# A two-round mixer trunk on one core: the second round's first head as two Strassen quads in turn, and a later gate for the last convolution group

## The chip, the cores and the metric

The kernel runs on one core of a Trainium2 chip. Its five engines are TensorE (PE, matmuls), VectorE (DVE), ScalarE (ACT), GpSimd (POOL) and SyncE (SP, which here issues transfers). The metric is the device time of one execution in microseconds. Before the change the median of three runs is 867.72 us.

## The reference

One layer of a hybrid trunk, all in fp32, for 2048 rows behind 16 meta tokens:

```python
hn = rms_norm(h, norm_g)
proj = hn @ w_in                                   # (rows, 1024) x (1024, 8*512)
cx, cb, cc, cg, q, k, v, rg = split(proj, 8)
conv_out = cb * causal_conv3(cc * cx) * silu(cg)   # 4 groups of 128 channels
q, k = rotary(q) * 128**-0.5, rotary(k)            # 4 heads of 128
ret = head_group_norm(retention_chunkwise(q, k, v), ret_norm_g)   # chunks of 128
mixed = concat(conv_out, ret * silu(rg))
out = rms_norm(h + mixed @ w_out, final_g)
```

## The kernel before

**Rounds and units.** The 2048 rows are worked in two rounds of 1024 (`NR`), and each round goes through eight units, four heads (0 to 3) and four convolution groups (4 to 7), in the order of `UNITS` (L37): round 0 starts with group 4, round 1 with head 0, and both end with group 7. Behind them come eight output pairs of 256 rows (`output`, L943). `rr` and `rr2` are a round's row factors of the norm; they are multiplied in behind the projection.

**Quads.** A unit projects 1024 rows on 2 x 256 columns. Each half of that, a quad, is a 2 x 2 problem of blocks with four k-tiles each. A weight tile is 128 x 512, a moving tile 128 x 512 (the rows). Each fp32 product is three fp32r matmuls, high and low parts against each other, so that a block product is 4 x 3 = 12 matmuls. `quad` (L241) does the four output blocks in seven products by Strassen's scheme in Winograd's form, 84 matmuls at L252. It needs sums of blocks on both sides, four of them for the weights (`stationary`, L147) and four for the moving side. `quad_plain` (L298) does eight products without sums, 96 matmuls at L309. Only the opening group of round 0, the first quad of round 1 (K and V of head 0) and output pair 0 are plain.

**Parts.** A weight is split by ACT (cast to `wh`, L119) and DVE (`wl`, L120) into a ring of three pairs (`RING`). The moving parts `mh{i}{kt}` and `ml{i}{kt}` (operand i, k-tile kt) have one buffer each and stay for the round. For round 1, `moving` (L182) loads 16 blocks of `x` with the gain (`ml` at L123), and `prepared` (L226) loads 16 sums (`sums_x`, made in round 0) as tiles `t`. The weights' sums of round 0 are kept in DRAM (`sums_a`) for round 1. A product's bank `pj` (four in PSUM) is copied by ACT to a `tc` (L259) or taken by DVE.

**The first head of round 1.** Its first quad is handed plain weights (`first`, L1140), `between[1]` (`rest_of_sums`, L1144) makes operands 3 and 4 of the moving side behind it, and the second quad (Q, RG) follows with operands 0 to 6. In `head` (L765), `take` (L776) puts K through `rotary` (L721, four DVE products) and V through `part` (L741: ACT splits the fp32 words into 16-bit planes, a transposing DMA `cross` turns them). Of the steps of the second quad, `split_keys` sends a half of K the same way, `join` puts a turned half of V together, `weigh` scales it, and `join_keys` makes `kd` in one of the two buffers of tag `b` (`brief`, L104). All this is ACT's.

**Group 7.** The second quad of `conv_group` (L649) gives the gate's two blocks (j = 0, 1) and the two of CB. `take` (L693) adds and scales a gate block (DVE), `gated` (L687) applies Silu (ACT) and multiplies the taps `cs[j]`, tiles named `c`, by `rr` and by the gate (two POOL products, `mul` at L663). In round 0 `store` waits in `kept` and is popped in `rest_of_sums`; in round 1 it follows at once.

**What sets the order.** No order is written by hand. The tile framework runs the program against a simulated timeline and gives each engine its instructions in the order that comes out; `tc.issue_after(ins)` holds a step behind an instruction. General tiles (`gen`, 16 buffers) carry loads, `u`, `c`, `kv`, `qg` and the rest.

The central lines of the program before, at the start of round 1:

```python
m, b = moving(load_x(r), gain_of)
first = [plain_parts(w_loads(0))]
load_tables()
prepared(m, sums_x, (1, 3))

def rest_of_sums():
    prepared(m, sums_x, (0, 2))
    with tc.issue_after(loaded[0].ins):
        kept.pop()()
```

Of the kernel before, what the change touches and what calls it, by code (L numbers as in the profile page):

```python
# [15 lines left out]
P = 128  # L16
# [4 lines left out]
NG = 4  # L21
# [57 lines left out]
def hybrid_trunk(ctx: ExitStack, tc: tile.TileContext, t, out: bass.AP, chunk_decay):  # L79
# [102 lines left out]
    def moving(load, scale=None, after={}, behind={}):  # L182
# [12 lines left out]
        return m, blocks  # L195

    def block_sums(b11, b12, b22, b21, t1, t3, f, g):
# [14 lines left out]
        sub(nc.vector, t3, b22, b11)  # L212
# [28 lines left out]
    def quad(w, m, take, steps=()):  # L241
# [42 lines left out]
        product(6, xb, False)  # L284
        take(1, 0, xb, None)

    def plain_part(n, load, slot):
# [151 lines left out]
    def row_factors(r, f):  # L439

        f.extend([row_tile("rr", r), row_tile("rr2", r), []])
        rows = load_rows(r, 0)
# [114 lines left out]
    def kept_sums(n, r):  # L557
        return sums_a[n] if r == 0 and n in KEPT else None

    mixed = [  # L560
# [88 lines left out]
    def conv_group(g, r, m, f, blocks, ahead, steps=(), last=False):  # L649
# [35 lines left out]
        gates = []  # L685

        def gated():  # L687
            j, c = gates.pop()
            nc.scalar.activation(c, c, AF.Silu)  # L689
            mul(nc.gpsimd, cs[j], cs[j], rr[j])  # L690
            mul(nc.gpsimd, cs[j], cs[j], c)

        def take(i, j, pp, c):  # L693
            if i == 0:
                add(nc.vector, c, pp, c)
# [44 lines left out]

    def part(a, to_cross=None):  # L741

        apart, across = gen("pl")[:, :HB], gen("tr")[:, :HB]
        nc.scalar.copy(out=planes(apart), in_=halves(a))
        if to_cross is None:
            cross(across, apart)
        else:
            to_cross.append((across, apart))
        return across
# [15 lines left out]
    def head(h, r, m, rot_t, f, turning, blocks, ahead, sums, first=(), between=((), idle, idle, idle)):  # L765
# [3 lines left out]

        to_cross, queried = [], []  # L770
        k, v, late = [None, None], [None, None], []
# [3 lines left out]

        def take(i, j, pp, c):  # L776
            if i == 1 and c is None:
                v[j] = part(pp, to_cross if len(first) else None)
                return
# [11 lines left out]

        if len(first) > 0:
            quad_plain(first[0], m, take)
        else:
            with tc.issue_after(spreading[0].ins) if r + h == 0 else nullcontext():
                w = stationary(blocks[0], nc.vector if r + h == 0 else nc.gpsimd, kept_sums(2 * h, r))
            quad(w, m, take, between[0] or (finish_late,))
            catch_up(0)
        between[1]()
        if to_cross:  # L800
            with tc.issue_after(loaded[0].ins):
                for pair in to_cross:
                    cross(*pair)
        q, sg = [None, None], [None, None]

        def take(i, j, pp, c):
            d = gen("qg")[:, :HB]
# [23 lines left out]

        def split_late():
            for j in late:
                v[j] = part(v[j])
            split_keys(0)

# [18 lines left out]

        quad(stationary(load_raw(w_loads(2 * h + 1, r)), keep=kept_sums(2 * h + 1, r)), m, take, (split_late, middle, late_middle))
        with tc.issue_after(copied[0].ins):
            join(1)
            weigh(1)
            join_keys(1)  # L860
        between[2]()
        with tc.issue_after(queried[0].ins):
# [80 lines left out]
    def output(pair, m, final_g):  # L943
# [111 lines left out]
    for r in range(NR):  # L1055
# [82 lines left out]
        else:  # L1138
            m, b = moving(load_x(r), gain_of)
            first = [plain_parts(w_loads(0))]  # L1140
            load_tables()
            prepared(m, sums_x, (1, 3))

            def rest_of_sums():  # L1144
                prepared(m, sums_x, (0, 2))
                with tc.issue_after(loaded[0].ins):
                    kept.pop()()

            between = (), rest_of_sums, idle, idle
            blocks = None, None  # L1150
# [5 lines left out]
        for n, unit in enumerate(units):  # L1156
# [67 lines left out]
```

## Time and profile before

| | |
|---|---|
| runs | 867.62, 867.72 and 867.89 us |
| profiled execution | 867.66 us, its span 865.9 us |
| PE | 854.1 us busy, 99% of the span, 4216 matmuls |
| DVE | 683.0 us, 79% |
| ACT | 499.0 us, 58% |
| POOL | 288.7 us, 33% |
| chain that ended last | PE 93%, DVE 3% |
| granted clock of PE | 0.998 on the mean |

Times run from the span's start. A busy PE row is a matmul's length as it is modelled, and neighbouring rows overlap; the distance between their starts is what PE spends on one. The first head of round 1 begins at about 360 us, and the output at about 710 us. "Released by" names what ended the idle time before an instruction.

### The profile page before, as it was taken

Reading aid. Unit: us, or ns where it says so; the run is one execution under the profiler, and the core shown is the slowest. Engines: PE = TensorE matmul, PEld = TensorE weight load, DVE = VectorE, ACT = ScalarE, POOL = GpSimd, SP = SyncE. Lnnn points to the kernel's source line nnn. Section 1 sums busy time; section 2 is a strip of 40 time slices with the busy share of each in tenths; the row PEclk is TensorE's granted clock in tenths of the full one; section 3 lists DMA queues with packets and bytes.
Section 4 is the critical chain, followed back from the end, with each engine's and each line's share of the span. In section 5 each row is a group of like instructions: output and inputs, shape, how many; then the busy total and the mean of one; then the engine's idle time right before and its main releaser. Section 6 shows DMA issues by size and latency. Waiting matters only on the chain.

```text
span 865.9 us, 12846 instructions
## 1 busy us (share of the span) xinstructions
PE 854.1 (99%) x4216; PEld 705.7 (82%) x4216; DVE 683.0 (79%) x1204; ACT 499.0 (58%) x901; POOL 288.7 (33%) x226
## 2 busy tenths in 40 slices
PE   8999999999999999999999999999999999999996
PEld 6778888878887778788888888888888888888885
DVE  6798989889897977979677787976655699767663
ACT  7875648474855654948374757544433565555553
POOL 0022232422255554320000002341312154777773
PEclk9999999999999999999999999999999999999999
DMA  8736357566777744966365657547344584455441
GB/s 294 252 142 159 96 145 210 149 185 193 183 233 242 243 147 158 338 197 163 81 171 178 162 194 167 186 135 256 97 122 122 205 318 146 162 181 169 146 139 68
DMA packets 141187, 154.43 MB, mean 178 GB/s; under 512 B 59904, under 2 KB 77632, under 8 KB 141120
## 3 DMA queue, kind: packets, MB, share of 16 engines
q1 hardware_dynamic: 140544, 153.21, 57.8%
q8 instruction: 33, 0.54, 0.3%
q10 hardware_dynamic: 576, 0.40, 0.1%
q14 instruction: 34, 0.28, 0.1%
HBM read 101.14 MB, written 39.85 MB: 163 GB/s over the span
## 4 chain that ended last, share of the span: by engine, by line
PE 93%; DVE 3%; issue 1%; DMA 1%; POOL 0%; ACT 0%; POOLq 0%; SPq 0%; DVEq 0%
PE pj L252 75%; PE pj L309 5%; PE pj L333 5%; PE ms L902 2%; PE ms L891 2%; PE ms L901 2%; PE ms L878 2%; PE ms L506 1%; DVE wl L120 1%; DMA ra<-in_w_in 1%; DVE ml L123 0%; DMA gain<-in_norm_g 0%; DVE qg L931 0%; DVE x L205 0%; DVE c L581 0%
## 5 line engine op out<-in xcount | busy, mean ns | idle before, releaser
L252 PE MATMUL pj<-mh,wl 128*128 128x512 f32 x1008 | 395.7, 393 | 0.5 <-DVE wl L120 0.5
L252 PE MATMUL pj<-mh,wh 128*128 128x512 f32 x1008 | 393.2, 390 | 0.0
L252 PE MATMUL pj<-ml,wh 128*128 128x512 f32 x1008 | 392.7, 390 | 0.0
L119 ACT CAST wh<-ra 128x512 fp32r<-128x512 f32 x229 | 142.3, 621 | 250.3 <-PE pj L252 210.6
L120 DVE TENSOR_TENSOR wl<-ra,wh 128x512 fp32r<-128x512 f32 x229 | 188.3, 824 | 59.4 <-ACT wh L119 58.2
L252 PEld LDWEIGHTS pj<-mh,wl 128*128 128x128 f32 x1008 | 189.3, 188 | 41.1 <-issue 1.1
L252 PEld LDWEIGHTS pj<-mh,wh 128*128 128x128 f32 x1008 | 189.3, 188 | 39.4
L252 PEld LDWEIGHTS pj<-ml,wh 128*128 128x128 f32 x1008 | 189.4, 188 | 38.1
L131 POOL TENSOR_TENSOR ra<-ra 128x512 f32<-128x512 f32 x44 | 69.0, 1567 | 78.7 <-PE ms L506 38.3
L914 POOL TENSOR_TENSOR rp<-rs,neg_half 128x4 f32<-128x4 f32 x16 | 18.8, 1173 | 151.5 <-DVE rs L128 151.4
L259 ACT COPY tc<-pj 128x512 f32<-128x512 f32 x108 | 62.6, 580 | 0.2
L128 POOL TENSOR_TENSOR sa<-ra 128x512 f32<-128x512 f32 x22 | 33.2, 1508 | 59.2 <-DMA ra<-in_w_in 38.2
L663 POOL TENSOR_TENSOR c<-c,tc 128x512 f32<-128x512 f32 x14 | 26.1, 1862 | 47.7 <-ACT tc L689 47.7
L131 POOL TENSOR_TENSOR ra<-sa,ra 128x512 f32<-128x512 f32 x22 | 31.7, 1440 | 30.5 <-DVE wl L120 20.6
L977 DVE TENSOR_TENSOR yo<-pj,yo 128x512 f32<-128x512 f32 (+1 forms) x33 | 21.9, 671 | 17.5 <-PE pj L252 8.8
L663 POOL TENSOR_TENSOR c<-c,rr 128x512 f32<-128x512 f32 x14 | 22.3, 1592 | 36.9 <-DVE c L704 25.0
L988 POOL TENSOR_TENSOR z<-yo,final_g 128x512 f32<-128x512 f32 x16 | 27.1, 1692 | 19.4 <-DVE yo L977 19.4
L128 DVE TENSOR_TENSOR tc<-pj,tc 128x512 f32<-128x512 f32 x28 | 19.2, 684 | 14.6 <-PE pj L252 14.6
L918 DVE TENSOR_SCALAR pm<-ms,mv,rp 128x128 f32<-128x128 f32 x64 | 21.8, 404 | 10.2 <-POOL rp L914 10.2
L123 DVE SCALAR_TENSOR_TENSOR ml<-x,gain,mh 128x512 fp32r<-128x512 f32 x32 | 24.7, 809 | 5.6 <-ACT mh L122 5.4
L128 POOL TENSOR_TENSOR yo<-yo,tc 128x512 f32<-128x512 f32 x18 | 26.0, 1454 | 3.4 <-ACT tc L259 3.2
L581 DVE SCALAR_TENSOR_TENSOR c<-u,conv_w,c 128x512 f32<-128x512 f32 x32 | 25.2, 830 | 2.3 <-POOL u L572 1.2
(161 smaller groups left out, 1214.0 us busy)
## 6 DMA issues: line engine op xcount, KB each, us to landing
ra<-in_w_in SPq DMA_DIRECT2D x111, 256.0 KB, 2.9
ra<-sums_a SPq DMA_DIRECT2D x52, 256.0 KB, 2.9
x<-in_xT SPq DMA_DIRECT2D x48, 256.0 KB, 5.0
sums_a<-ra SPq DMA_DIRECT2D x42, 256.0 KB, 2.1
w<-in_w_out SPq DMA_DIRECT2D x32, 256.0 KB, 5.0
ra<-mixed SPq DMA_DIRECT2D x32, 256.0 KB, 2.8
yo<-in_x SPq DMA_DIRECT2D x32, 256.0 KB, 4.4
ra<-in_x SPq DMA_DIRECT2D x16, 256.0 KB, 3.5
```

What stands on the lines that cost most here:

```text
L119: nc.scalar.copy(out=hi, in_=src)
L120: lowered[0] = eng.tensor_tensor(out=lo, in0=src, in1=hi.bitcast(F32), op=ALU.subtract)
L123: nc.vector.scalar_tensor_tensor(out=lo, in0=src, scalar=scale, in1=hi.bitcast(F32), op0=ALU.mult, op1=ALU.subtract)
L128: eng.tensor_tensor(out=out, in0=a, in1=b, op=ALU.add)
L131: eng.tensor_tensor(out=out, in0=a, in1=b, op=ALU.subtract)
L252: nc.tensor.matmul(bank, a[:, ks], b, start=first and kt == 0 and n == 0, stop=kt == KH - 1 and n == 2, skip_group_check=not first,)
L259: copied[0] = nc.scalar.copy(out=c, in_=bank)
L309: nc.tensor.matmul(banks[i], a[:, ks], b, start=half + kt + n == 0, stop=half == 1 and kt == KH - 1 and n == 2,)
L333: nc.tensor.matmul(banks[n][i], a[:, ks], b, start=half + kt + s == 0, stop=half == 1 and kt == KH - 1 and s == 2,)
L581: nc.vector.scalar_tensor_tensor(out=c, in0=u[:, tap : tap + HB], scalar=conv_w[:, g, tap : tap + 1], in1=c, op0=ALU.mult, op1=ALU.add)
L663: eng.tensor_tensor(out=out, in0=a, in1=b, op=ALU.mult)
L988: nc.gpsimd.tensor_tensor(out=ys[i][j], in0=y, in1=final_g[:, j * HB : (j + 1) * HB], op=ALU.mult)
```

## The change

**The head.** `moving` and the plain weights go at the start of round 1. `moving_in_turn` loads operands 0 and 1 of the moving side and hands back five steps that make operands 2, 3, 4, 5 and 6. The new `quads` runs both quads of head 0 product by product, K/V's and then Q/RG's, seven products each, and does a step behind each pair of products. All four banks are in use. `weights_in_turn` splits a quad's weights one by one as its products ask for them; K/V now takes its sums from `sums_a`, which Q/RG did already. Key and value splits are steps as well, and joins and weighings come behind the last product.

**Group 7.** `last` is now true in both rounds. Then the gate's addition goes to a `brief("cg")`, and nothing more is done. `gate_late` does the rest: per j a product of the gate with `rr` (DVE, L732), Silu (ACT), a product of the taps with `rr` (DVE instead of POOL, also L732), and their product (POOL). It returns `store`. Round 0's stands in the step that makes operand 6 in round 1's head (`gate_kept`), round 1's at the end of output pair 1.

```diff
+    def moving_in_turn(load, scale, sums):
...
+        blocks(0, 0)
+        blocks(1, 0)
+        steps = [
+            lambda: sums(m, 1), lambda: sums(m, 0), lambda: sums(m, 2), lambda: blocks(1, 1), lambda: sums(m, 3),
+        ]
+        return m, steps
...
+    def quads(ws, m, takes, between=()):
...
+        for i in range(7):
+            for n, take in enumerate(takes):
+                if i < 2:
+                    banks[n][i] = ps_proj()
+                bank = banks[n][1 if i in (1, 3, 5) else 0]
+                product(n, i, bank, i in (0, 1, 3))
...
+            next(between, idle)()
...
+    def weights_in_turn(n, r):
+        for load in w_loads(n, r):
+            a = raw()
+            load(a)
+            yield weight_parts(a)
...
         def take(i, j, pp, c):
             if i == 0:
+                if last:
+                    gate = brief("cg")
+                    add(nc.vector, gate, pp, c)
+                    ungated.append(gate)
+                    return
...
+        def gate_late():
+            for j, gate in enumerate(ungated):
+                mul(nc.vector, gate, gate, rr[j])
+                nc.scalar.activation(gate, gate, AF.Silu)
+                mul(nc.vector, cs[j], cs[j], rr[j])
+                mul(nc.gpsimd, cs[j], cs[j], gate)
+            return store
+
         if last:
-            kept.append(store)
+            kept.append(gate_late)
...
-        if len(first) > 0:
-            quad_plain(first[0], m, take)
...
+        if len(first) > 0:
+            steps = list(first) + [split_values, lambda: split_keys(1)]
+            steps[3] = lambda: (first[3](), split_keys(0))
+            quads([weights_in_turn(2 * h + n, r) for n in range(2)], m, (take_keys, take_queries), steps)
+            join_keys(0)
             join(1)
             weigh(1)
+            join(0)
+            weigh(0)
             join_keys(1)
+        else:
...
+        if pair == 1:
+            with tc.issue_after(last[0].ins):
+                kept.pop()()()
...
-            m, b = moving(load_x(r), gain_of)
-            first = [plain_parts(w_loads(0))]
+            m, first = moving_in_turn(load_x(r), gain_of, lambda m, n: prepared(m, sums_x, (n,)))
             load_tables()
-            prepared(m, sums_x, (1, 3))
...
+            def gate_kept(last=first[4]):
+                last()
+                with queued((loaded[0], lowered[0])):
+                    kept.pop()()()
+
+            first[4] = gate_kept
+            between = (), idle, idle, idle
...
-                blocks = conv_group(unit - NG, r, m, f, blocks, rest, FACTOR_STEPS.get(unit, ()) if r == 0 else (), r == 0 and following is None)
+                blocks = conv_group(unit - NG, r, m, f, blocks, rest, FACTOR_STEPS.get(unit, ()) if r == 0 else (), following is None)
```

**The order, first piece.** DVE late in round 1's first head, where the last moving parts and weights are made (`wl` weights, `ml30` operand 3's tile 0, `kv` and `qg` rotary products). Before:

```order
L727 TENSOR_TENSOR kv_4150<-kv_4150,rot_t_3868 128x512
L728 TENSOR_TENSOR kv_4150<-kv_4150,rot_4152 128x512
L120 TENSOR_TENSOR ml30_4163<-t_4160,mh30_4162 128x512
L120 TENSOR_TENSOR ml31_4169<-t_4166,mh31_4168 128x512
L120 TENSOR_TENSOR wl_4239<-ra_4218,wh_4238 128x512
L120 TENSOR_TENSOR ml32_4175<-t_4172,mh32_4174 128x512
L120 TENSOR_TENSOR ml33_4181<-t_4178,mh33_4180 128x512
L120 TENSOR_TENSOR ml40_4187<-t_4184,mh40_4186 128x512
```

And with the change:

```order
L814 TENSOR_TENSOR qg_4025<-qg_4025,rot_4027 128x512
L120 TENSOR_TENSOR wl_4191<-ra_4188,wh_4190 128x512
L120 TENSOR_TENSOR ml41_4105<-t_4102,mh41_4104 128x512
L120 TENSOR_TENSOR ml42_4111<-t_4108,mh42_4110 128x512
L120 TENSOR_TENSOR ml43_4117<-t_4114,mh43_4116 128x512
L123 SCALAR_TENSOR_TENSOR ml50_4163<-x_4160,gain_69,mh50_4162 128x512
L123 SCALAR_TENSOR_TENSOR ml51_4169<-x_4166,gain_69,mh51_4168 128x512
L123 SCALAR_TENSOR_TENSOR ml52_4175<-x_4172,gain_69,mh52_4174 128x512
L123 SCALAR_TENSOR_TENSOR ml53_4181<-x_4178,gain_69,mh53_4180 128x512
L120 TENSOR_TENSOR wl_4211<-ra_4208,wh_4210 128x512
```

Operands 4 and 5 now stand ahead of the weight `wl_4211`, the fifth of the Q/RG quad; before, weights and operand 3 alternated, and operand 5 had been made ahead of the head.

**The order, second piece.** DVE at the end of that head, up to the next quad's first weights (`wl_4496` before, `wl_4485` with the change; `cg` the kept gate, `c` the taps, `qg` tiles of Q and RG). Before:

```order
L128 TENSOR_TENSOR qg_4346<-pj_4254,tc_4326 128x512
L820 TENSOR_TENSOR qg_4346<-qg_4346,rr_2970 128x512
L120 TENSOR_TENSOR wl_4496<-ra_4390,wh_4495 128x512
L128 TENSOR_TENSOR qg_4361<-pj_4313,tc_4305 128x512
L120 TENSOR_TENSOR wl_4500<-ra_4392,wh_4499 128x512
L725 TENSOR_TENSOR rot_4363<-qg_4361,rot_t_3868 64x512
```

And with the change:

```order
L732 TENSOR_TENSOR cg_3790<-cg_3790,rr_360 128x512
L732 TENSOR_TENSOR c_3682<-c_3682,rr_360 128x512
L732 TENSOR_TENSOR cg_3847<-cg_3847,rr_360 128x512
L732 TENSOR_TENSOR c_3686<-c_3686,rr_360 128x512
L128 TENSOR_TENSOR qg_4306<-pj_4006,tc_4094 128x512
L120 TENSOR_TENSOR wl_4485<-ra_4379,wh_4484 128x512
L813 TENSOR_TENSOR kv_4281<-kv_4281,rot_t_3862 128x512
L891 TENSOR_TENSOR qg_4357<-pj_3935,rr_2971 128x512
L120 TENSOR_TENSOR wl_4489<-ra_4381,wh_4488 128x512
```

Four gate products at L732 now stand ahead of the last addition of Q and of the next quad's first weight.

**The order, third piece.** DVE at the turn from output pair 1 to pair 2 (`yo` a block of the output; `wl_7662` before and `wl_7653` with the change are pair 2's third weight). Before:

```order
L977 TENSOR_TENSOR yo_7454<-pj_7499,yo_7454 128x512
L1012 SCALAR_TENSOR_TENSOR yo_7452<-yo_7452,rf_7613,final_g_7198 128x512
L120 TENSOR_TENSOR wl_7662<-ra_7640,wh_7661 128x512
L128 TENSOR_TENSOR tot_7621<-so_7449 128x1
L345 TENSOR_SCALAR rs_v_7624<-tot_7621 128x1
L1012 SCALAR_TENSOR_TENSOR yo_7454<-yo_7454,rf_7623,final_g_7198 128x512
```

And with the change:

```order
L1068 TENSOR_TENSOR yo_7435<-pj_7480,yo_7435 128x512
L732 TENSOR_TENSOR cg_7011<-cg_7011,rr_2971 128x512
L732 TENSOR_TENSOR c_6933<-c_6933,rr_2971 128x512
L732 TENSOR_TENSOR cg_7068<-cg_7068,rr_2971 128x512
L732 TENSOR_TENSOR c_6937<-c_6937,rr_2971 128x512
L1106 SCALAR_TENSOR_TENSOR yo_7433<-yo_7433,rf_7604,final_g_7179 128x512
L120 TENSOR_TENSOR wl_7653<-ra_7631,wh_7652 128x512
```

The same four products of round 1's gate stand ahead of the scaling of `yo` (L1012 before, L1106 now) and of that weight.

## Rows read from the trace of the kernel before

**Rows 1.** Page, section 1: busy time and share of the span, instructions of each engine
```profile
PE 854.1 (99%) x4216; PEld 705.7 (82%) x4216; DVE 683.0 (79%) x1204; ACT 499.0 (58%) x901; POOL 288.7 (33%) x226
```

**Rows 2.** Table by stretches: PE, PEld, DVE, ACT, POOL busy us (instructions), clock, DMA share, GB/s
```profile
600.00:620.00 20.00, 20.00 (x90) 16.57 (x89) 12.65 (x18) 7.85 (x14) 4.88 (x5) 1.00 0.47 148
700.00:720.00 20.00, 20.00 (x90) 16.57 (x89) 20.00 (x25) 9.41 (x17) 10.23 (x7) 1.00 0.64 231
```

**Rows 3.** Chain of waits, 350 to 410 us: start, us, what
```profile
360.69 0.69 DVE ml L120
...
388.70 19.04 PE pj L252 x84
```

**Rows 4.** PE's timeline at the head: start, us, engine, line [idle before <-releaser]
```profile
360.02 0.39 PE L309 MATMUL pj<-mh,mh 128*128 128x512 f32 x1
361.42 0.50 PE L309 MATMUL pj<-mh,ml 128*128 128x512 f32 x1 [1.02 <-DVE ml L120]
```

**Rows 5.** DVE's timeline at the head, 353 to 376 us
```profile
353.87 0.74 DVE L123 SCALAR_TENSOR_TENSOR ml<-x,gain,mh 128x512 fp32r<-128x512 f32 x1
354.53 0.68 DVE L663 TENSOR_TENSOR tc<-tc,rr 128x512 f32<-128x512 f32 x1
355.13 0.68 DVE L120 TENSOR_TENSOR wl<-ra,wh 128x512 fp32r<-128x512 f32 x1
...
374.31 0.69 DVE L725 TENSOR_TENSOR rot<-kv,rot_t 64x512 f32<-64x512 f32 x1
...
375.72 0.75 DVE L123 SCALAR_TENSOR_TENSOR ml<-x,gain,mh 128x512 fp32r<-128x512 f32 x1
```

**Rows 6.** DVE's, POOL's timelines, 351 to 385 us; a stretch; POOL's products (min/median/max ns)
```profile
351.55 1.79 DVE L120 TENSOR_TENSOR wl<-sa,wh 128x512 fp32r<-128x512 f32 x1
...
351.05 1.74 POOL L663 TENSOR_TENSOR c<-c,rr 128x512 f32<-128x512 f32 x1 [1.64 <-DVE c L581]
...
379.81 5.16 POOL L663 TENSOR_TENSOR c<-c,tc 128x512 f32<-128x512 f32 x1 [11.02 <-ACT tc L689]
...
379.81:384.97 5.16, 5.16 (x25) 4.26 (x24) 4.01 (x7) 0.00 (x0) 5.16 (x1) 1.00 0.57 184
...
L663 POOL TENSOR_TENSOR c<-c,rr x12: 1292/1712/2346, 310.1 to 703.8; 128x512 f32<-128x512 f32 x12
L663 POOL TENSOR_TENSOR c<-c,tc x12: 1287/1296/5158, 315.7 to 713.0; 128x512 f32<-128x512 f32 x12
```

**Rows 7.** DMA issues, 372 to 412 us, then 345 to 400: KB each, us to landing
```profile
t<-sums_x SPq DMA_DIRECT2D x8, 256.0 KB, 2.8
...
t<-sums_x SPq DMA_DIRECT2D x16, 256.0 KB, 4.8
...
tr<-pl SPq DMA_TRANSPOSE x3, 3.1
```

**Rows 8.** ACT's timeline at the head's end, 397 to 404 us
```profile
397.21 0.62 ACT L119 CAST wh<-ra 128x512 fp32r<-128x512 f32 x1
397.74 0.57 ACT L259 COPY tc<-pj 128x512 f32<-128x512 f32 x1
398.21 1.35 ACT L839 COPY v<-tr 128x1024 uint16<-128x1024 uint16 x1
399.43 1.03 ACT L744 COPY pl<-kv 128x1024 uint16<-128x1024 uint16 x1
...
401.37 1.28 ACT L845 ACTIVATE v<-v,vk 128x128 f32<-128x128 f32 x4
402.55 1.34 ACT L830 COPY kd<-tr 128x1024 uint16<-128x1024 uint16 x1
```

**Rows 9.** Timelines of DVE, then PE, at the end of output pair 1
```profile
745.82 0.75 DVE L1012 SCALAR_TENSOR_TENSOR yo<-yo,rf,final_g 128x512 f32<-128x512 f32 x1 [1.09 <-POOL rf L348]
746.49 0.69 DVE L120 TENSOR_TENSOR wl<-ra,wh 128x512 fp32r<-128x512 f32 x1
...
743.41 0.39 PE L252 MATMUL pj<-mh,wl 128*128 128x512 f32 x1
```

More of the change, by code (lines that the diff above doesn't have):

```diff
@@ L195, in moving, with blocks @@
         return m, blocks
+    def moving_in_turn(load, scale, sums):
+        m = [[] for _ in range(8)]
+        def blocks(half, j):
+            for kt in range(KH):
+                k = half * KH + kt
+                parts(m, BLOCK[half][j], kt, load(k, j), scale(k) if scale else None)
+        blocks(0, 0)
[4 more added lines that the diff above has]
+        return m, steps
     def block_sums(b11, b12, b22, b21, t1, t3, f, g):
@@ L285, in quad, with product, copy @@
         take(1, 0, xb, None)
+    def quads(ws, m, takes, between=()):
+        between = iter(between)
+        banks = [[None, None] for _ in ws]
+        copies = [None for _ in ws]
+        def product(n, i, bank, first):
+            wh, wl = next(ws[n])
+            for kt in range(KH):
+                ks = slice(kt * P, (kt + 1) * P)
+                mh, ml = m[i][kt]
+                for s, (a, b) in enumerate(((wl, mh), (wh, ml), (wh, mh))):
+                    nc.tensor.matmul(
+                        bank, a[:, ks], b, start=first and kt == 0 and s == 0, stop=kt == KH - 1 and s == 2,
+                        skip_group_check=not first,
+                    )
+        def copy(bank):
+            c = sb.tile([P, HB], F32, name="tc", tag="tc", bufs=COPIES)
+            copied[0] = nc.scalar.copy(out=c, in_=bank)
+            return c
+        for i in range(7):
[4 more added lines that the diff above has]
+                product(n, i, bank, i in (0, 1, 3))
+                if i == 0:
+                    copies[n] = copy(bank)
+                elif i == 1:
+                    take(0, 0, bank, copies[n])
+                elif i == 2:
+                    copies[n] = [copy(bank)]
+                elif i == 3:
+                    copies[n].append(copy(bank))
+                elif i == 4:
+                    take(1, 1, bank, copies[n][1])
+                elif i == 5:
+                    take(0, 1, bank, copies[n][0])
+                else:
+                    take(1, 0, bank, None)
+            next(between, idle)()
     def plain_part(n, load, slot):
@@ L439, in row_factors @@
     def row_factors(r, f):
-        f.extend([row_tile("rr", r), row_tile("rr2", r), []])
+        rr2 = row_tile("rr2", r)
+        f.extend([row_tile("rr", r), rr2, []])
         rows = load_rows(r, 0)
@@ L685, in conv_group @@
         gates = []
+        ungated = []
         def gated():
+            if last:
+                return
             j, c = gates.pop()
@@ L694, in take @@
             if i == 0:
+                if last:
+                    gate = brief("cg")
+                    add(nc.vector, gate, pp, c)
+                    ungated.append(gate)
+                    return
                 add(nc.vector, c, pp, c)
@@ L739, in cross, with part @@
         )
-    def part(a, to_cross=None):
+    def part(a):
         apart, across = gen("pl")[:, :HB], gen("tr")[:, :HB]
         nc.scalar.copy(out=planes(apart), in_=halves(a))
[L745 to L748, printed above, removed]
+        cross(across, apart)
         return across
@@ L774, in head, with take_keys @@
         tables = [rot_t[:, :, j * HB : (j + 1) * HB] for j in range(2)]
-        def take(i, j, pp, c):
+        def take_keys(i, j, pp, c):
             if i == 1 and c is None:
-                v[j] = part(pp, to_cross if len(first) else None)
+                v[j] = part(pp)
                 return
@@ L790, in take, with take_queries @@
                 late.append(j)
-        if len(first) > 0:
-            quad_plain(first[0], m, take)
[L794 to L803, printed above, removed]
         q, sg = [None, None], [None, None]
-        def take(i, j, pp, c):
+        def take_queries(i, j, pp, c):
             d = gen("qg")[:, :HB]
@@ L830, in join_keys, with split_values, split_late @@
             nc.scalar.copy(out=halves(kt[j]), in_=planes(across_k[j]))
-        def split_late():
+        def split_values():
             for j in late:
                 v[j] = part(v[j])
+        def split_late():
+            split_values()
             split_keys(0)
@@ L854, in late_middle @@
             between[3]()
-        quad(stationary(load_raw(w_loads(2 * h + 1, r)), keep=kept_sums(2 * h + 1, r)), m, take, (split_late, middle, late_middle))
-        with tc.issue_after(copied[0].ins):
+        if len(first) > 0:
[3 more added lines that the diff above has]
+            join_keys(0)
             join(1)
             weigh(1)
+            join(0)
+            weigh(0)
             join_keys(1)
+        else:
+            with tc.issue_after(spreading[0].ins) if r + h == 0 else nullcontext():
+                w = stationary(blocks[0], nc.vector if r + h == 0 else nc.gpsimd, kept_sums(2 * h, r))
+            quad(w, m, take_keys, between[0] or (finish_late,))
+            catch_up(0)
+            between[1]()
+            w = stationary(load_raw(w_loads(2 * h + 1, r)), keep=kept_sums(2 * h + 1, r))
+            quad(w, m, take_queries, (split_late, middle, late_middle))
+            with tc.issue_after(copied[0].ins):
+                join(1)
+                weigh(1)
+                join_keys(1)
         between[2]()
```

7 lines of the change are left out of this document (1 added, 6 removed).

## The prediction

> **What bounds the kernel now.** I first read the page's busy shares [rows 1]: TensorE (PE) is busy for 99% of the span, VectorE (DVE) for 79%, ScalarE (ACT) for 58%, GpSimd (POOL) for 33%. A matmul's end is modelled, so I read PE by its starts. The table by stretches [rows 2] shows 90 matmuls of 512 columns in 20 us both at 600 to 620 and at 700 to 720, the second with DVE busy for all 20 us: PE keeps its pitch beside a full DVE, and a matmul taken away there is time. The granted clock is 1.00 in each stretch, the higher of the two levels (2.4 GHz), and PE does not fall idle, so the clock stays out of the sum. The pitch is in the chain of waits [rows 3]: 84 matmuls in 19.04 us, 0.2267 us each, so a product of twelve takes 2.72 us. The chain also shows the one wait of note at the change: before 361.42 it goes through DVE, not PE. PE's timeline [rows 4] has a matmul at 360.02 and the next at 361.42, released by DVE's `ml`: 1.40 less 0.23, PE lost 1.17 us. From there to 407.74 it runs through.
>
> **What goes.** (a) The first head had 96 + 84 matmuls and now has 84 + 84: 12 x 0.2267 = 2.72 us, all on the path. (b) The wait at 360.02 goes. It came because 23 matmuls of the plain quad stood ahead of the last two products of the convolution group, and their `ml` parts were late. Now those two products come first (360.02 to 365.46), and at 365.46 the head needs eight `x` parts and one weight, not sixteen and four. From 353.87 the new DVE order has eight instructions with the gain (pitch 0.66) and ten others (0.60) up to the head's first weight [rows 5]: 353.87 + 5.3 + 6.0 = 365.2, in time by 0.3. POOL's two gate products of this stretch are gone as well; the one at 351.05 held a DVE instruction back by 1.1 us, 1.79 us for a `wl` where 0.68 is usual [rows 6]. So I count all of the 1.17. The transfers (four `x` loads less, four kept sums more) cost nothing while 256 KB land in about 3 us [rows 7] and are asked for a product or more ahead. Sum of what goes: 3.9 us.
>
> **What comes, term c: weight 4 of the second quad.** The 14 products now start every 2.72 us from 365.46, K/V and Q/RG in turn, and DVE makes 13 of the 14 weights and 16 of the 28 moving parts meanwhile. Weight 3 of K/V takes the buffer of Q/RG's product 1, which ends at 365.46 + 4 x 2.72 = 376.34; with ACT's cast (0.62) and DVE's subtraction its `wl` ends at about 378.3. From there to `wl_4211` (weight 4 of Q/RG) the new order has twenty DVE instructions (the first order piece shows the last of them): fourteen at 0.60, a rotary pair of 1.41, four with the gain at 0.66 [rows 5]: 8.4 + 1.4 + 2.6 = 12.4, so 390.7. PE wants it at 365.46 + 9 x 2.72 = 389.95 and waits at least 0.8 us. Counted from the load of operand 3's first part (asked for at 375.7, behind weight 2; landed at 378.7, through ACT and DVE at 379.9; then 11.3 us on DVE) it is 1.3. I take 1.3, as the later of the two chains decides. Ends: 0.8, and 2.5 if that load takes 4.8 us, as in the crowded stretch [rows 7].
>
> **Term d: the kept gate at the end of the head.** Four products for the gate now stand on DVE ahead of the first weight of the next quad (second order piece). From the end of K/V's product 5 DVE needs 0.7 for its addition, ten instructions of 0.60 and a rotary pair: 8.1 us. PE wants that weight after three more products, 8.16 us. It is a tie, and POOL decides it, for its two gate products come in just here. A POOL product beside dense DVE work delays an instruction with two SBUF operands by up to 1.1 us [rows 6]. The first holds back the fourth gate product by 1.2; the second begins while an addition from PSUM runs and holds back the weight by 0.7: 1.9 us. Ends: 0, if POOL falls into gaps, and 2.6, the price of rival 2's first product. I take 1.9, since the order has no gap there. Behind it ACT has a key split, two weight casts, a bank copy, two joins, two weighings, a key join, a cast and a bank copy, 9.6 us [rows 8] (each 0.1 less than its row, as neighbours overlap), from 2.3 us after the head's end: 12.0 us. PE wants that bank after four products and eleven small matmuls, 12.1 us. That just holds.
>
> The Trainium skill, "SBUF — State Buffer", section "SBUF: two separate sides", says that a VectorE instruction with two SBUF inputs and a GpSimd instruction that reads SBUF exclude each other for the whole instruction, whichever starts first. The row of 1.79 us agrees. The POOL product of 5.16 us [rows 6] does not: seven DVE instructions, 4.01 us in all, ran beside it. By that rule alone term d would be 1.9 and rival 2 out; by the row rival 2 keeps a chance.
>
> **Term e: the kept gate in the output.** In round 1 the same four products go to the end of output pair 1, ahead of weight 2 of pair 2 (third order piece). Before, that `wl` ended at 747.18 [rows 9]; PE wants it at 743.41 + 2 x 2.72 = 748.85. The four, 2.4 us, fill DVE's wait of 1.09 us for `rf` and push it to 748.5: in time by 0.3. If POOL's first gate product gets in ahead of it, it is 1.1 later, and PE waits 0.8. I take 0.4, ends 0 and 0.8. The stretch that loses work, 700 to 720, gains nothing, as PE keeps its pitch there already [rows 2].
>
> **Sum:** -2.72 - 1.17 + 1.3 + 1.9 + 0.4 = -0.3 us. The profiled execution took 867.66 (span 865.9), 0.06 under the median of the runs, 867.72. So 867.4. A measurement of this kernel can tell about 0.2%, 1.7 us, from no change: this is no change.
>
> **Rivals.** 1. DVE's new work stays hidden: POOL falls where DVE waits for PE anyway, d and e are 0, and c alone stands: -3.9 + 1.3 = -2.6, 865.1 us (864.6 with c at 0.8). For it: PE does not feel a full DVE at 700 to 720 [rows 2], and a tie needs half a microsecond to vanish. Against: rows 6, and an order without gaps. It holds as long as c + d + e stay under 2.2.
>
> 2. POOL is held out instead of DVE, as in the product of 5.16 us. The key joins write the two buffers that hold the gates, so ACT's first key join waits for POOL's first product; and the stores of the gated blocks stand in SP's queue ahead of the transposed copy of the second key half. From the end of POOL's second product it is a store, three loads and that copy (3.1 us to land, rows 7; 4.8 with the issues ahead of it), then key join, weighing, cast and bank copy (3.5 us, again rows 8) until PE has its bank. So if that product ends over 3.8 us after the head does (in my count it ends before), every further microsecond is PE's. With both at 5.16 us it ends 8.7 after, PE waits 0.4 for a weight behind the first join and 4.5 for the bank, and the sum is -3.9 + 1.3 + 4.9 + 0.8 = +3.1: 870.8 us. From 7.3 us after the head's end on, the whole is slower by over 0.2%. For it: two of the 24 products of this kind from 300 us on took over 4 us; against: the medians of their two kinds are 1.71 and 1.30 [rows 6].
>
> 3. That the matmuls stay is out: PE's new order has twelve rows fewer, all at this head.
>
> **How the numbers follow.** The forecast, within 1.7 us of 867.7, gets 0.53: two firm gains against three waits, of which one is firm. Rival 1 gets 0.32, as d and e are ties and a wait can't be less than 0 but can fail to come. Rival 2 gets 0.15, milder forms with late loads included. The forecast's own range is 866.0 to 869.4. For 8 in 10 the range goes down to 864.7, nearly all of rival 1, and up to 869.3, which leaves out the far part of rival 2. So faster by over 0.2%: 0.32; within 0.2%: 0.53; slower by over 0.2%: 0.15.
>
> **What would show it.** Right: 12 matmuls fewer; no wait of PE where the head begins; one of 0.8 to 1.3 us ahead of the head's tenth product, released by `wl`; one of 1 to 2 us at the first product of the next quad, with a DVE instruction of about 1.8 us and POOL's product beside it; at most 0.8 us in output pair 2. If the head's 168 matmuls run through in 38.1 us and the next quad follows at once, rival 1 holds, and c and d fail. If a gate product on POOL takes over 4 us and PE waits for ACT's bank copy ahead of the next quad's product 4, it is rival 2. A wait for `mh` or `ml` in operands 3 or 6 of the head would say that I mis-sized the loads.

## The result and the profile after

The change makes the kernel slower: 871.49 us, median of 6 runs (869.75 to 874.14), against 867.81 before. The ratio is 1.0044, with a 95% interval from 1.0031 to 1.0057. A second batch of the same kernel gave 1.0052 (1.0035 to 1.0069). That lies outside the forecast range of 864.7 to 869.3.

The page's busy shares after the change, against [rows 1]:

```profile
PE 851.8 (98%) x4204; PEld 702.8 (81%) x4204; DVE 686.8 (79%) x1210; ACT 499.6 (58%) x901; POOL 274.8 (32%) x222
```

The twelve matmuls are gone (4216 to 4204), and with them 2.3 us of PE's busy time; but PE is busy for 98% of the span, not 99%. So the loss is waits. PE's timeline has them, as in [rows 4]: the idle time before a matmul, and what ended it.

```profile
360.32 0.50 PE L269 MATMUL pj<-mh,wl 128*128 128x512 f32 x1 [1.08 <-ACT tc L276]
...
392.13 0.50 PE L317 MATMUL pj<-mh,wl 128*128 128x512 f32 x1 [1.60 <-DVE wl L120]
...
408.36 0.50 PE L269 MATMUL pj<-mh,wl 128*128 128x512 f32 x1 [2.33 <-DVE wl L120]
...
750.93 0.47 PE L269 MATMUL pj<-mh,wl 128*128 128x512 f32 x1 [1.23 <-DVE wl L120]
...
762.31 0.50 PE L269 MATMUL pj<-mh,wl 128*128 128x512 f32 x1 [0.22 <-DVE yo L1068]
```

PE lost the idle time and 0.16 us more (the row ahead is modelled with 0.39 us, the pitch is 0.23): 1.24 us at 360.32, 1.76 at 392.13, 2.49 at 408.36, 1.39 at 750.93 and 0.38 at 762.31. Before, it lost 1.17 at 361.42 and nothing at the other places. The chain of waits through the first head, against [rows 3]:

```profile
357.53 0.62 ACT mh L122
...
359.67 0.60 ACT tc L276
...
360.32 5.74 PE pj L269 x24
366.05 10.89 PE pj L317 x48
...
377.99 5.70 DMA t<-sums_x
...
390.73 0.64 DVE ml L123
...
391.39 0.70 DVE wl L120
...
392.13 8.48 PE pj L317 x36
...
404.35 1.70 DVE c L732
...
406.58 1.74 DVE wl L120
...
408.36 3.71 PE pj L269 x15
```

Product numbers count from 0. The first wait comes through ACT (the bank copy `tc` at 359.67, on a queue full of casts such as the `mh` at 357.53). It holds up the last convolution group's product 5, and the head starts two products later. The second is taken back by the chain to a load of the kept sums (operand 4's first part, 5.70 us), through DVE's `ml` to a `wl`. The third is two DVE instructions of 1.70 and 1.74 us.

The whole from the first steady matmuls to the last: 815.16 us before, 818.86 after in the profiled execution, +3.70. By the waits it is -2.72 - 1.17 + 1.24 + 1.76 + 2.49 + 1.39 + 0.38 = +3.37; the other 0.3 us have no single place. The profiled execution's span is only 2.1 us longer than before, since its first loads came 1.0 us sooner and its tail behind the last matmul was 0.6 us shorter, neither of which the change touches. It is also the shortest of the six runs: at 869.75 us it lies 1.7 us under their median, so its waits are not all that the median has to explain.

### The profile page after: what moved, and what is told of

The parts are those of the page before. It is cut to its first block, busy times and chain, and to the rows that moved or that the text cites. A ratio compares the mean times of both kernels' runs of the same rounds, so it can differ in the third digit from the quotient of the medians.

```text
span 868.0 us, 12816 instructions
## 1 busy us (share of the span) xinstructions
PE 851.8 (98%) x4204; PEld 702.8 (81%) x4204; DVE 686.8 (79%) x1210; ACT 499.6 (58%) x901; POOL 274.8 (32%) x222
## 4 chain that ended last, share of the span: by engine, by line
PE 90%; DVE 4%; DMA 2%; ACT 1%; issue 1%; POOL 0%; SPq 0%; ACTq 0%; POOLq 0%; DVEq 0%
PE pj L269 72%; PE pj L395 5%; PE pj L371 3%; PE pj L317 2%; PE ms L993 2%; PE ms L982 2%; PE ms L992 2%; PE ms L969 2%; DVE wl L120 1%; PE ms L569 1%; DMA t<-sums_x 1%; DMA x<-in_xT 1%; DMA out_y<-z 0%; DMA ra<-in_w_in 0%; DVE c L732 0%
## 5 line engine op out<-in xcount | busy, mean ns | idle before, releaser
L269 PE MATMUL pj<-mh,wl 128*128 128x512 f32 x980 | 385.0, 393 | 5.3 <-DVE wl L120 4.0
L269 PE MATMUL pj<-mh,wh 128*128 128x512 f32 x980 | 382.4, 390 | 0.0
L269 PE MATMUL pj<-ml,wh 128*128 128x512 f32 x980 | 381.9, 390 | 0.0
L120 DVE TENSOR_TENSOR wl<-ra,wh 128x512 fp32r<-128x512 f32 x236 | 195.5, 831 | 60.5 <-ACT wh L119 58.9
L269 PEld LDWEIGHTS pj<-mh,wl 128*128 128x128 f32 x980 | 184.1, 188 | 46.2 <-DVE wl L120 2.8
L269 PEld LDWEIGHTS pj<-mh,wh 128*128 128x128 f32 x980 | 184.0, 188 | 38.2
L269 PEld LDWEIGHTS pj<-ml,wh 128*128 128x128 f32 x980 | 184.1, 188 | 37.2
L120 DVE TENSOR_TENSOR ml<-t,mh 128x512 fp32r<-128x512 f32 x32 | 24.6, 803 | 1.9 <-ACT mh L119 1.6
L830 ACT COPY pl<-kv 128x1024 uint16<-128x1024 uint16 x24 | 24.7, 1043 | 1.8 <-DVE kv L814 1.8
L395 PE MATMUL pj<-mh,mh 128*128 128x512 f32 x64 | 25.0, 401 | 0.8 <-ACT mh L1179 0.8
```

The source lines that it names most:

```text
L120: lowered[0] = eng.tensor_tensor(out=lo, in0=src, in1=hi.bitcast(F32), op=ALU.subtract)
L269: nc.tensor.matmul(bank, a[:, ks], b, start=first and kt == 0 and n == 0, stop=kt == KH - 1 and n == 2, skip_group_check=not first,)
L395: nc.tensor.matmul(banks[n][i], a[:, ks], b, start=half + kt + s == 0, stop=half == 1 and kt == KH - 1 and s == 2,)
```

## The experiments

Theory after the first trace: four waits, each with a cause of its own. (b) ACT's bank copy comes late ahead of the head. (c) The fifth weight of Q/RG stands behind too much on DVE. (d), (e) Each late gate costs by POOL's products more than by DVE's. The rival in each case: the engines are full, so that a fix only moves the wait.

All kernels, as ratios to the kernel before on the same chip:

| kernel | median us | ratio (95%) |
|---|---|---|
| changed / again | 871.49 / 872.68 | 1.0044 (1.0031 to 1.0057) / 1.0052 (1.0035 to 1.0069) |
| copy_first | 870.94 | 1.0032 (1.0019 to 1.0045) |
| weight_first | 870.97 | 1.0031 (1.0019 to 1.0042) |
| loads_early | 868.85 | 1.0013 (1.0004 to 1.0021) |
| gate_dve | 867.61 | 0.9999 (0.9988 to 1.0010) |
| no_late_out | 870.54 | 1.0029 (1.0018 to 1.0040) |
| gate0_back | 868.69 | 1.0009 (1.0000 to 1.0019) |
| gates_back | 866.47 | 0.9987 (0.9978 to 0.9995) |
| late_out | 868.86 | 1.0010 (1.0001 to 1.0019) |
| best_back | 865.75 | 0.9972 (0.9961 to 0.9983) |
| best_dve | 865.16 | 0.9967 (0.9954 to 0.9979) |
| best_mix | 865.62 | 0.9975 (0.9966 to 0.9985) |

### b: the wait ahead of the head

copy_first, on the change (in `moving_in_turn`; `copy` is `copied[0]` on entry, the last bank copy of the convolution group):

```diff
+        def behind(step):
+            with tc.issue_after(copy.ins):
+                step()
+
         blocks(0, 0)
-        blocks(1, 0)
+        behind(lambda: blocks(1, 0))
         steps = [
-            lambda: sums(m, 1),
+            lambda: behind(lambda: sums(m, 1)),
...
```

> The casts of operands 1 and 2 for the new head are held behind the bank copy of the last convolution group's product 3. Theory (four waits of PE, each with its own cause; this one is ACT's: that copy stood behind five casts and came 3.3 us after its product): the wait of 1.24 us ahead of that group's product 5 goes, the other three stay, and the time is 871.5 - 1.2 = 870.3 us. Rival (ACT and DVE are full here, so the work only moves): operand 1 or 2 comes late instead, PE waits about as much at the head's third or fifth product, and the time stays at 871.5.

Why the copy was late is in ACT's timeline of the change:

```profile
355.36 0.57 ACT L276 COPY tc<-pj 128x512 f32<-128x512 f32 x1
355.84 0.73 ACT L122 ACTIVATE mh<-x,gain 128x512 fp32r<-128x512 f32 x1
356.46 0.57 ACT L444 COPY rr<-ms 128x512 f32<-128x512 f32 x1
356.93 0.60 ACT L446 ACTIVATE rr<-ms 128x512 f32<-128x512 f32 x1
357.41 1.34 ACT L122 ACTIVATE mh<-x,gain 128x512 fp32r<-128x512 f32 x2
358.64 0.62 ACT L119 CAST mh<-t 128x512 fp32r<-128x512 f32 x1
359.15 0.62 ACT L119 CAST wh<-ra 128x512 fp32r<-128x512 f32 x1
359.67 0.59 ACT L276 COPY tc<-pj 128x512 f32<-128x512 f32 x1
```

The copy of product 2 is at 355.36. Product 3 ended at 356.36 on PE, but its copy runs 3.3 us later, at 359.67, since casts of `x` and `t`, a weight's cast and two instructions for row factors stand ahead of it, and ACT has not a gap. In copy_first it ran in time (`tc` at 357.32), and the wait turned up two products later, at the head's first matmul (1.40 us). The chain of copy_first there:

```profile
357.41 0.48 ACT tc L281
...
362.40 1.89 DVE ml L120 x3
364.30 0.60 DVE cg L128
364.90 0.60 DVE ml L120
365.49 0.61 DVE wl L120
...
366.15 1.89 PE pj L322 x7
```

From 358.5 on DVE runs without a gap, with operand 2 (`ml` at 362.40 and 364.90) ahead of the head's first weight (`wl` at 365.49). The rival was right that the wait only moves, though it named the head's third or fifth product and not its first. Part of this is the edit's own doing: while operand 1's casts were held back, DVE idled for 1.46 and 0.41 us ahead of 358.5. weight_first keeps operand 1 behind the copy, loads operand 2's sums where they were, and holds the parts of operands 2 and 3 (n is 1 and 0) behind a weight:

```diff
...
+                with tc.issue_after(lowered[0].ins) if n < 2 else nullcontext():
+                    prepared(m, sums_x, (n,), early)
```

> The casts of operand 1 stand behind the bank copy, as in copy_first, and those of operands 2 and 3 behind the first and second weights of the Q/RG quad. Theory, mended after copy_first (there the copy was in time, but DVE still ran without a gap from 358.5 to 366 us with operand 2 ahead of the head's first weight, so the wait only moved): with operand 2 behind that weight the head starts without a wait, while the waits at the tenth product, at the head's end and in the output stay: 871.5 - 1.2 = 870.3 us. Rival (what DVE must do up to the head's first weight is too much in any order, or operand 2 is late now): the wait stays near 1.3 us at the head's first or fifth product, 871 to 871.5 us.

In its trace the head starts without a wait; the three later ones stand (1.42, 2.49, and 1.39 with 0.38). In the times this is not settled: 1.0031 lies below the change's two ratios by 0.13 and 0.21%, where 0.14% was expected, but the intervals overlap. (best_back and best_dve, below, rest on the same edit and start the head with 0.41 us of wait and with none.)

### c: the tenth product of the head

loads_early asks for operand 3's sums right behind operand 2's:

```diff
+            def in_turn(m, n):
+                prepared(m, sums_x, (n,), early)
+                if n == 1:
+                    for kt in range(KH):
+                        a = early[0, kt] = gen("t")[:, :HB]
+                        nc.sync.dma_start(a, sums_x[0, kt])
```

> The four kept sums of operand 3 are loaded one step earlier, right behind those of operand 2. Theory (the wait at the head's tenth product starts with these loads, which were asked for only at 377 us and landed 5.7 us later, and DVE then had too much in a row): operand 3 is made while DVE idles at 367 to 374, the wait of 1.76 us goes to 0 to 0.8, and the time is 869.7 to 870.6 us. Rival (DVE's total work in the head is the bound, whatever the order): the wait stays near 1.8 us or turns up one product later, 871.5.

The wait is gone; in the chain of loads_early the weight is ready at 387.90 and PE runs on for 70 matmuls:

```profile
387.20 0.70 DVE wl L120
...
387.94 16.22 PE pj L317 x70
```

The time fell by 0.31 to 0.39%, more than the 1.76 us (0.20%) that the first trace showed there, and the interval allows both; it came out below the expected 869.7 to 870.6. (The wait ahead of the head was 0.77 us in this trace instead of 1.24, without an edit there.) So the wait was one of order and not of DVE's total: DVE had been idle for 2 us at a time between 367 and 374 us, while the loads stood in SP's queue behind weights that waited for buffers.

### d and e: the late gates

> The last product of each late gate runs on DVE instead of POOL, in both rounds; DVE gets four more products of 0.6 us. Theory (POOL's products each hold a DVE instruction back by 1.1 us, two at the head's end and two in output pair 2): DVE instructions of 1.7 to 1.8 us disappear from both places, the wait at the next quad's first weight falls from 2.5 to 0.3 us, those in the output from 1.8 to 0.2, and the time is about 867.8 us. Rival (the four products with the row factor, standing ahead of the weight, are the price): the waits stay at 1.3 us or more at the head's end and 0.7 in the output, 869.7 us or more.

```diff
-                mul(nc.gpsimd, cs[j], cs[j], gate)
+                mul(nc.vector, cs[j], cs[j], gate)
```

At the head's end the changed kernel has this, DVE's timeline first and POOL's behind it:

```profile
403.67 0.69 DVE L732 TENSOR_TENSOR cg<-cg,rr 128x512 f32<-128x512 f32 x1
404.27 1.79 DVE L732 TENSOR_TENSOR c<-c,rr 128x512 f32<-128x512 f32 x1
405.98 0.68 DVE L128 TENSOR_TENSOR qg<-pj,tc 128x512 f32<-128x512 f32 x1
406.58 1.73 DVE L120 TENSOR_TENSOR wl<-ra,wh 128x512 fp32r<-128x512 f32 x1
...
403.89 1.61 POOL L732 TENSOR_TENSOR c<-c,cg 128x512 f32<-128x512 f32 x1 [55.42 <-ACT cg L794]
406.49 1.27 POOL L732 TENSOR_TENSOR c<-c,cg 128x512 f32<-128x512 f32 x1 [0.98 <-DVE c L732]
```

Two DVE instructions of 0.68 become 1.79 and 1.73, one for each POOL product that was already running. With the products on DVE the same stretch is:

```profile
404.12 0.69 DVE L732 TENSOR_TENSOR c<-c,rr 128x512 f32<-128x512 f32 x1
404.73 0.68 DVE L128 TENSOR_TENSOR qg<-pj,tc 128x512 f32<-128x512 f32 x1
405.33 0.68 DVE L120 TENSOR_TENSOR wl<-ra,wh 128x512 fp32r<-128x512 f32 x1
...
406.53 1.29 DVE L732 TENSOR_TENSOR c<-c,cg 128x512 f32<-128x512 f32 x2
```

The wait falls from 2.49 to 0.34 us, though DVE has two products more (the pair at 406.53 comes behind the weight). The output's wait of 1.39 goes too; that of 0.38 is still there, with 0.57, at the same matmul (now at 760.05). The time is the forecast one, 867.6 against 867.8, but not wait by wait: new are waits of 0.36 us at 418.82 and 0.34 at 694.00, both for ACT, and the one ahead of the head is 0.57 instead of 1.24. In the output of the changed kernel the pattern at the `wl` had been the same, both of POOL's products running while DVE scaled `yo` and made the weight:

```profile
746.72 0.68 DVE L732 TENSOR_TENSOR c<-c,rr 128x512 f32<-128x512 f32 x1
747.32 1.78 DVE L1106 SCALAR_TENSOR_TENSOR yo<-yo,rf,final_g 128x512 f32<-128x512 f32 x1
749.03 1.76 DVE L120 TENSOR_TENSOR wl<-ra,wh 128x512 fp32r<-128x512 f32 x1
...
747.17 3.07 POOL L732 TENSOR_TENSOR c<-c,cg 128x512 f32<-128x512 f32 x2 [1.97 <-ACT cg L794]
```

The Trainium skill, "SBUF — State Buffer", section "SBUF: two separate sides", has a VectorE instruction with two SBUF inputs and a GpSimd one that reads SBUF exclude each other for the whole instruction, whichever came first. These rows agree for DVE: each of the four long instructions ends 0.55 us after the POOL product beside it, as though it had begun only then. In gate_dve a POOL addition beside the two products took 3.05 us, and 1.30 in the kernel before, so POOL is held too. Its row and the last DVE instruction beside it, then the last of the seven beside the product of 5.16 us in the kernel before [rows 6]:

```profile
748.85 0.69 DVE L120 TENSOR_TENSOR wl<-sa,wh 128x512 fp32r<-128x512 f32 x1
747.64 3.05 POOL L128 TENSOR_TENSOR yo<-yo,tc 128x512 f32<-128x512 f32 x1 [3.48 <-ACT tc L276]
...
383.13 0.69 DVE L728 TENSOR_TENSOR kv<-kv,rot 128x512 f32<-128x512 f32 x1
```

POOL ends 1.15 us behind DVE both times (750.69 and 749.54, 384.97 and 383.82), a little under the shortest time of such a product on POOL (1.27 to 1.30). So the row of 5.16 us, which the prediction read against the rule, fits the exclusion as well. What it does not fit is the order: POOL, once held, was passed by several DVE instructions that came after it. Why DVE was held in one place and POOL in the other isn't shown.

Then the gates were undone one by one: in both rounds (gates_back), in round 1 alone (no_late_out), in round 0 alone (gate0_back); late_out puts round 1's late gate alone into the kernel before. The edits restore the old lines of `conv_group` for the round in question; for round 0, gate0_back:

```diff
         def gated():
-            if last:
+            if last and r:
                 return
...
-                if last:
+                if last and r:
                     gate = brief("cg")
...
-            kept.append(gate_late)
+            kept.append(gate_late if r else store)
...
-                    kept.pop()()()
+                    kept.pop()()
```

and for round 1, no_late_out:

```diff
-        if pair == 1:
-            with tc.issue_after(last[0].ins):
-                kept.pop()()()
...
-                blocks = conv_group(unit - NG, r, m, f, blocks, rest, FACTOR_STEPS.get(unit, ()) if r == 0 else (), following is None)
+                blocks = conv_group(unit - NG, r, m, f, blocks, rest, FACTOR_STEPS.get(unit, ()) if r == 0 else (), r == 0 and following is None)
```

> The head runs as changed, but both late gates are undone: group 7 gates on the spot in both rounds, as before the change. Theory: the waits at the next quad's first weight (2.5 us) and in the output (1.8 us) go; those of 1.24 and 1.76 us stay, the first up to 1.1 us longer as POOL's gate products return beside it: 871.5 - 4.3 = 867.2, up to 868.3 us. Rival (the head itself has no slack left on DVE, so any order waits about as long): still 870 us or more.

> The change without its part in the output: round 1's gate on the spot, round 0's late as changed. Theory by the first trace: the waits of 1.4 and 0.4 us in output pair 2 go, 871.5 - 1.8 = 869.7 us. Rival (late_out was only 0.7 us above the kernel before, so a usual run pays less there than the profiled one): 870.8 us.

> The change without round 0's late gate: group 7 of round 0 gates on the spot, round 1's gate stays in output pair 1. Theory: the wait of 2.5 us at the head's end goes, and the fall of the clock behind it, 1 us on the mean; the wait ahead of the head grows by 0.6 us as in gates_back: 871.5 - 2.5 - 1.0 + 0.6 = 868.6 us. gates_back minus this kernel is then the price of the late gate in the output, 0.7 to 1.8 us, so 867.2 to 868.3 by that way. Rival (no fall of the clock in the usual run): 869.6 us.

> The kernel before, with one part of the change alone: round 1's last convolution group gets its gate at the end of output pair 1, with POOL's products as in the change. Theory: this alone brings the waits in output pair 2 (1.4 and 0.4 us), with a scaling of yo and a wl of 1.8 us each beside POOL's two products: 867.9 + 1.8 = 869.7 us. Rival (the output is late only because the head has shifted what stands around it): no new wait, 867.9 us.

The four corners agree: each late gate costs the same with the other and without it, within 0.03%. Head alone: 0.9987, a gain of 1.1 us. Round 0's late gate adds 0.42% (gates_back to no_late_out) or 0.39% (gate0_back to the mean of the change's two ratios, 1.0048), about 3.5 us. Round 1's adds 0.22% or 0.19%, about 1.8 us. (That -1.1 + 3.5 + 1.8 gives the 4.2 us of 1.0048 follows from how these were taken.) Of the times, gate0_back came as expected (868.69 for 868.6). gates_back came 0.7 us under its range, and no_late_out at 870.54, nearer to its rival's 870.8 than to 869.7, though its ratio lies 0.19% below the change's, 1.7 us where 1.8 was expected. In the traces, over the last 648 matmuls PE takes 148.9 to 149.1 us in the seven with the late gate there on POOL, 146.9 in the four with it on the spot and 147.1 before. late_out alone was a miss in its time, 0.7 us where 1.8 was expected (interval 0.1 to 1.6), though its trace has both waits, 1.39 and 0.55 us, and one of 0.66 at 695.56. That profiled execution, 870.24 us, was the second longest of 11; what the others did is not shown, and on the old head round 1's gate may cost less than on the new one.

### The clock behind the longest wait

> The changed kernel once more, for a second trace and more runs. Theory (the wait of 2.5 us at the head's end lets PE's granted clock fall in some executions, as it did behind the same wait in loads_early and weight_first, to 0.5 for 3 to 4 us, some 1.6 us of time; the first trace of the change was one without it): the median is again 870.5 to 872 us, the granted clock of its runs goes from 0.998 down to 0.996, and the runs with the lower clock are the longer ones by 1 to 2 us. Rival (the runs above the profiled one wait longer at the same places): no tie between clock and time.

In weight_first, behind the same wait of 2.5 us, the table by stretches shows PE at half clock (columns as [rows 2]):

```profile
403.86:406.58 2.72, 0.39 (x3) 0.00 (x1) 2.72 (x4) 2.70 (x4) 1.26 (x1) 0.99 0.49 133
406.58:409.70 3.12, 3.12 (x7) 2.48 (x8) 3.09 (x6) 1.29 (x3) 0.00 (x0) 0.50 0.99 226
```

Seven matmuls in 3.12 us where 1.59 is usual: 1.5 us more. In the first trace of the change the same stretch was undisturbed:

```profile
408.36:411.40 3.04, 3.04 (x13) 2.53 (x14) 3.01 (x6) 1.22 (x3) 0.00 (x0) 1.00 0.95 231
```

Of six traces with this wait three show the fall (loads_early, weight_first, no_late_out), three do not (the change twice, copy_first). The mean granted clock of single runs says how often: it is 0.996 or less in 21 of 46 runs of these kernels, and in 1 of 65 runs of the seven kernels whose wait there is at most 0.4 us. In the repeat the clock went from 0.998 (870.26, 870.30 and 872.90 us) to 0.994 (872.96 and 874.62): a tie, not a strict one, since other waits vary by up to a microsecond as well (one that ends at 297.65, long ahead of the changed head, was 1.57 us here and 0.61 in the first trace; one of 0.63 at 385.68 is new). The median, 872.68, lies above the 872 expected at most. In each of the six kernels the runs at 0.996 or less are the longer ones on the mean, by 0.4 to 2.2 us. The mean clock is a sign and not a measure: the profiled run of loads_early, which shows the fall, has 0.997, and a run of no_late_out with 0.946 took 871.04 us, no longer than its neighbours.

This is a part of what round 0's late gate costs beyond its wait. An estimate: 1.5 us in 21 of 46 runs is 0.7 us on the mean. The wait of 2.49 less the 0.6 to 0.8 us by which the one ahead of the head is shorter with the late gate (1.24, 1.33 and 1.06 against 1.87 and 1.93), and 0.7, make about 2.5 of the 3.5 us. The remaining microsecond isn't placed.

### A version faster than both

best_back, best_dve and best_mix put the moves of weight_first and loads_early together, on gates_back, on gate_dve, and on gate_dve with round 1's gate on the spot.

> gates_back (both gates on the spot), with operand 1 behind the bank copy, operands 2 and 3 behind the Q/RG quad's first two weights, and operand 3's sums loaded with operand 2's. Theory: its two waits that are left, 1.87 us ahead of the convolution group's product 5 and 1.5 us at the head's tenth product, go: 866.5 - 3.4 = 863.1 us, up to 864.3 if POOL's gate products still hold DVE back by 1.1 us ahead of the head. Rival (at the head's start POOL's products are the bound): the first wait stays, 865 us.

> gate_dve (late gates, all of them on DVE), with the same three moves as best_back. Theory: waits of 0.6 and 1.9 us go, 867.6 - 2.5 = 865.1 us; what is left above best_back is the late gate itself: 0.3 us at the head's end, 0.4 behind it and 0.9 in the output. Rival (the late gate frees POOL and DVE ahead of the head, and that is worth more than it costs): at or below best_back.

> best_dve with round 1's gate on the spot, as before the change; round 0's late gate stays, all on DVE. Theory (a late gate pays ahead of the head, where DVE and POOL are full, and costs in the output): the waits of 0.6 us in output pair 2 and at 692 us go, 864.5 us, the fastest of all. Rival (the gate on the spot costs round 1's last group as much): 865.2 us, like best_dve.

All three beat the kernel before by 0.25 to 0.33%, and can't be told from each other: best_dve came where it was expected. best_back came 1.5 us above the end of its range, 864.3, and near its rival's 865 (its trace has waits of 0.41, 0.31 and 0.79 us in the head), and best_mix 1.1 us above 864.5: its trace still has a wait of 0.80 us at 692.43, which was to go. So the prices that told them apart in the expectations were not confirmed. The chain of best_dve through the head's start is PE alone:

```profile
354.96 10.88 PE pj L271 x48
365.83 4.24 PE pj L319 x18
```

## Why the prediction was wrong

The sum failed term by term. Against the forecast -0.3 us, b is 1.24 us worse, c 0.46, d 0.59 and e 1.37, together 3.7 us, and that gives the first trace's +3.4. The rest, up to the 3.8 and 4.5 us of the two ratios, is in part the clock.

**a** held: twelve matmuls, 2.72 us.

**b** failed at "in time by 0.3" and so at "I count all of the 1.17". That count was DVE's alone. ACT, which makes the high part of every tile that DVE makes a low part of, had the same new order and no gap, and the bank copy that PE needs came 3.3 us after its product. Gain 0 instead of 1.17: the old wait went and one of 1.24 came. DVE's own count was about right. In the change's trace the head's first weight is

```profile
363.71 0.69 DVE L120 TENSOR_TENSOR wl<-ra,wh 128x512 fp32r<-128x512 f32 x1
```

and ends at 364.40; without the wait PE would have asked for it at about 364.5 (359.08 and 24 matmuls). (The `x` parts began at 351.8 where 353.87 was counted from, but idled up to 0.8 us for ACT.)

**c** was right in place and release (a `wl` ahead of the tenth product), and 1.76 in size where 1.3 was taken and 0.8 to 2.5 allowed. The load that the count went from, operand 3's first part, was asked for at 376.02 and took 3.00 us, as counted; the one of 5.70 us, which the chain names, is operand 4's. From the `ml` of operand 3's first part on,

```profile
379.70 0.69 DVE L120 TENSOR_TENSOR ml<-t,mh 128x512 fp32r<-128x512 f32 x1
```

DVE idled for 0.3 us at most up to the `wl` that PE waited for, so operand 4's load can have cost no more than that. The chain ended 0.9 us later than counted (392.1 for 391.2) and PE asked 0.4 later. loads_early confirms that the place of operand 3's loads decided.

**d** was right in mechanism: the fourth gate product held back (1.79), then the weight (1.73), 2.49 us where 1.9 was taken and 2.6 was the end. The two holds took 1.1 us each where 1.2 and 0.7 were counted, and the tie itself was missed by the 0.34 us that gate_dve still waits. But "the clock stays out of the sum" failed: it was argued from a PE that does not fall idle, and term d itself was the idle time. In all, round 0's gate costs 3.5 us, of which about one is not explained.

**e** failed in size: 0.4 was taken, 0.8 the end, 1.8 came. Both POOL products got in, not one, and each was paid, since the scaling of `yo` and the weight stand next to each other on DVE; and the yo chain behind it cost 0.4 more. (gate_dve has that last wait too, so it isn't POOL's products that make it.)

**The rivals.** Rival 1 asked for POOL to fall into gaps; none of the four products did. Rival 2 named the right side and the wrong mechanism: POOL's products took 1.61 and 1.27 us, no bank copy was late at the next quad, and the slowdown came from ordinary waits. One (b) had been put at nothing, c came inside its range, d near its bad end and e beyond it. All four erred the same way, while the sum took their middles as though the errors were independent. At b, d and e new work was put where ACT or DVE had no slack; c was a matter of order, as loads_early shows. The 0.15 for a slowdown stood with rival 2, so that the chance it gave to what happened was for another mechanism.

## What to carry to other kernels

Where a step is moved, count up each engine that touches it, to the instruction that PE waits for: a cast and its subtraction are two queues, and a bank copy stands in one of them. Near dense DVE work, count what an elementwise product given to POOL does to DVE: here each of four held a DVE instruction back by about 1.1 us, and DVE did the product itself in 0.6 us, which took the waits of 2.49 and 1.39 us down to 0.34 and none. And look at the granted clock of many runs, not only at one trace, where PE has come to wait: the wait may cost more than its length.

## What was not expected of the hardware

The granted clock fell from 1.00 to 0.50, 2.4 to 1.2 GHz, for some 3 us behind a wait of 2.5 us in three of six traces, at 1.5 us in the one shown. In the change's own two traces the same wait left it at 1.00, and the waits of up to 1.9 us ahead of the head and at its tenth product left it there in every trace. What decides between the two after equal waits isn't shown by these runs.
